# Causal masks of two attentions: 128 mask matmuls taken out, the mask moved to the scan and to GpSimd

## The chip, the cores and the metric

The kernel runs on one core of one Trainium2 chip. The metric is the device time of one execution in microseconds. The engines are named as in the profile: PE (TensorE, matmuls), PEld (its weight loads), DVE (VectorE), ACT (ScalarE), POOL (GpSimd) and SP (the queue that issues most DMAs).

## The reference

One decoder block on 1024 tokens of width 1024, in float32: eight heads of gated ("forgetting") attention and eight of stick-breaking attention side by side, attention to 256 memory tokens, and a convolutional gated FFN. Only the first part is touched:

```python
# gated heads, blocks of 128 queries
logits = q.k * scale + c[t] - c[s]          # c = cumsum(log f)
logits = where(s <= t, logits, -inf)
o = softmax(logits) @ v

# stick-breaking heads, strictly causal
z = q.k * scale
log_keep = where(s < t, log_sigmoid(-z), 0)
after = reverse_cumsum(log_keep) - log_keep  # over j > s
a = where(s < t, exp(log_sigmoid(z) + after), 0)   # sigmoid(z[t,s]) * prod_{s<j<t} (1 - sigmoid(z[t,j]))
o = a @ v
```

## The kernel before

Every float32 product is made of rounded parts: an operand is split into a high and a low part, ACT makes the high one and DVE the low one, and `mm3` (L201 to L203) adds three matmuls. The kernel has three stretches. From 0 to about 10 us it loads and normalises x. From there to about 612 us run the *planned steps*: both attentions, and between them, as background work for PE, the projections that make their queries, keys and values (`pq`, `pv`), those of the memory (`pk`, `pmv`) and half of the output projection (`pm`), which ends at about 640 us. Then come the rest of the output projection, the memory attention and the FFN.

The attention is cut into 32 groups: four pairs of heads (`pr`), for each first the gated kind ("f") and then the stick-breaking kind ("s"), two heads (`a`) and two halves of the queries (`g`). A group has four rows `i` of 128 queries; row `i` has 128 (i+1) keys, in chunks of at most 512. The steps of a row:

- `score` (L612, L613): two matmuls per chunk into a PSUM tile `st` (three of them). On the last chunk, which holds the diagonal block, a third matmul (L615) of a bfloat16 identity with a bfloat16 mask (0, or -1e30 above the diagonal) adds the mask to the last 128 columns.
- gated: `fox1` (L626) adds the gate row `negc` to the scores on DVE, writes them to SBUF as `p` and keeps the maximum in `fx`; L629 makes the negated maximum; `fox2` (L633) is the exponential on ACT with its sum; L588 the reciprocal on DVE; `fox3` (L636) the normalisation on POOL.
- stick-breaking: `sb1` (L644) and `sb2` (L647) are sigmoid(z) and sigmoid(-z) on ACT; `sb3` (L652) is a scan on DVE from the last column to the first, a running product that starts at 1; `sb4` (L658) multiplies sigmoid(z) by the scan shifted by one column, on POOL.

When its rows are done, a group turns them on PE (`turn`, L700), splits the result into high and low parts `pth` (L704) and `ptl` (L708), and multiplies by the values (`apply`, L716 and L717). Closing steps (L725 to L767) add the halves, split the result into `mh` and `ml` (which take tiles of `pth` and `ptl`) and store them.

The order of the work on each engine is written out by a planner: each step has an engine, a length, tiles that it takes and gives, and a due time `at`; a simulated run over these gives the order, and each engine then executes its own list, in that order, as the semaphores allow. One unit of due time is one group; `share` says how many us of background matmuls belong to each unit (about 8), `pace` deals them out, and R_STEP, T_OFF, T_LEN, W_LEAD and E_LEAD place the rows of a group, the turning, the loading of weights (`prep`: load L372, high L377, low L382) and the evacuations. The stretch ahead of the planned steps is ordered by a scheduler; there `get` (L189 to L195) loads and splits the first weights through three tiles `wraw`, and `norm_half` (L222 to L233) normalises two token tiles at a time and turns them on PE.

Of the kernel before, what the change touches and what calls it, by code (L numbers as in the profile page):

```python
# [133 lines left out]
def hybrid_block(ctx, tc, x, mem, w, wf, pcol, bfg, fing, out):  # L134
# [48 lines left out]
    def make_w(rp, wp):  # L183
        def get(i, eng=G):
            hi = wp.tile([P, 1024], F32R, tag="whi", name=f"whi{i}")
            lo = wp.tile([P, 1024], F32R, tag="wlo", name=f"wlo{i}")
            for c in (slice(0, 512), slice(512, 1024)):
                raw = rp.tile([P, 512], F32, tag="wraw", name=f"wraw{i}", bufs=3)
                in_turn("load", lambda: nc.sync.dma_start(raw, w[i, :, c]))  # L189
# [5 lines left out]
                in_turn("low", lambda: V.tensor_tensor(lo[:, c], raw, hi[:, c].bitcast(F32), op=ALU.subtract))  # L195
            return hi, lo
        return get
# [16 lines left out]
    def norm_half(src_tiles, gcol, hi, lo, pst, wk, n=4, tags=(("T", 2),), xtag="xn", eng=V):  # L214

        ss = small.tile([P, 4], F32, tag="ss", bufs=2, name="ss")
        rs = small.tile([P, 4], F32, tag="rs", bufs=2, name="rs")
        xn = []
        for j in range(n):
            xs = src_tiles[j]  # L220
            t = wk.tile([P, D], F32, tag=xtag, name="xn")
            A.activation(t, xs, AF.Square, accum_out=ss[:, j:j + 1])  # L222
            rsqrt_mean(rs[:, j:j + 1], ss[:, j:j + 1], 1, D)
            if eng is V:
                V.tensor_scalar(out=t, in0=xs, scalar1=rs[:, j:j + 1], scalar2=None, op0=ALU.mult)
# [52 lines left out]
    first_w = []  # L278
    hT = [half(0, 1, "h1_0"), half(2, 3, "h1_1")]
    with tc.tile_pool(name="nx", bufs=4, side="right", reuse_waits="tile") as nx:  # L280
        for th in range(2):
            xt = []
            for j in range(4):
                t = nx.tile([P, D], F32, tag="xin", name="xin")
                nc.sync.dma_start(t, x[(4 * th + j) * P:(4 * th + j + 1) * P, :])
                xt.append(t)
                if th == 0 and j % 2 == 1:
                    first_w.append(getw(ti))
# [4 lines left out]
            step = 2 if th else 2  # L293
            for j in range(0, 4, step):
                c = slice(j * P, (j + step) * P)
                norm_half(xt[j:j + step], C_ATTN, [t[:, c] for t in hT[th][0]], [t[:, c] for t in hT[th][1]],
                          ps, nx, n=step, tags=(("T", 2), ("S", 3)), eng=V if th == 0 else V)
# [11 lines left out]
        G.affine_select(out=mask_f, in_=zb, compare_op=ALU.is_ge, fill=NEG, base=0,  # L309
                        pattern=[[-1, P]], channel_multiplier=1)  # L310
        G.affine_select(out=mask_s, in_=zb, compare_op=ALU.is_ge, fill=NEG, base=-1,
                        pattern=[[-1, P]], channel_multiplier=1)
# [41 lines left out]
    def mm(n):  # L354
        return 30 * (n > 128) + n * 0.39 + 10
# [194 lines left out]
    negcs, kindend, before, stored, rms = {}, [], [None], {}, []  # L550

    class Group:
# [6 lines left out]
        def scores(self):  # L559
# [3 lines left out]
            for j in range(4):  # L563
# [7 lines left out]
                for n, (c0, w_) in enumerate(ch):  # L571
                    diag = c0 + w_ == n0
                    ms.append(plan.add(PE, 2 * mm(w_) + diag * mm(P), lambda i=i, c_=c_, n=n, c0=c0, w_=w_, diag=diag:
                                       self.score(i, c_, n, c0, w_, diag), need + ms,
# [4 lines left out]
                if kind == "f":  # L579
                    prev = [negcs[2 * pr + a]["in"]]  # L580
                    for n, (c0, w_) in enumerate(ch):
                        prev = [plan.add(DVE, 100 + dve(w_) + 130 * (n == len(ch) - 1),
                                         lambda i=i, c_=c_, n=n, c0=c0, w_=w_: self.fox1(i, c_, n, c0, w_),
                                         prev + [ms[n]], [],
                                         ["S"] + ["negc"] * (i == 7 and n == 1), at=at)]
                    e_ = plan.add(ACT, act(n0) + 95, lambda i=i, c_=c_, l=len(ch): self.fox2(i, c_, l), prev + kindend[-1:],
                                  at=at)
                    r_ = plan.add(DVE, 75, lambda c_=c_: V.reciprocal(c_["fx"][:, 3:4], c_["fx"][:, 3:4]), [e_], at=at)  # L588
                    o_ = plan.add(POOL, 100 + n0 * 1.05, lambda i=i, c_=c_: self.fox3(i, c_), [r_], [], ["fx"], at=at, lock=True)
                    last = e_  # L590
                else:
# [9 lines left out]
                    o_ = plan.add(POOL, 120 + n0 * 2.3, lambda i=i, c_=c_: self.sb4(i, c_), [s_] + pos, [], ["aw"], at=at,  # L601
# [6 lines left out]
        def score(self, i, c_, n, c0, w_, diag):  # L608
# [4 lines left out]
            T.matmul(st[:, :w_], lq, k2[:, c0:c0 + w_], start=False, stop=not diag)  # L613
            if diag:
                T.matmul(st[:, w_ - P:w_], identb, mask_f if self.kind == "f" else mask_s,  # L615
                         start=False, stop=True)
# [3 lines left out]

        def fox1(self, i, c_, n, c0, w_):
            if n == 0:
                self.row_tile(i, c_)
                c_["fx"] = small.tile([P, 4], F32, tag="fx", name="fx")
            mx, negc = c_["fx"][:, 0:2], negcs[2 * self.pr + self.a]["t"]
            V.tensor_tensor_reduce(out=c_["p"][:, c0:c0 + w_], in0=c_["st", n][:, :w_], in1=negc[:, c0:c0 + w_],  # L626
                                   scale=1.0, scalar=-3.0e38, op0=ALU.add, op1=ALU.max, accum_out=mx[:, n:n + 1])
            if c0 + w_ == P * (i + 1):
                V.tensor_scalar(out=c_["fx"][:, 2:3], in0=mx[:, 0:1], scalar1=mx[:, 1:2] if n else -3.0e38,  # L629
                                scalar2=-1.0, op0=ALU.max, op1=ALU.mult)  # L630

        def fox2(self, i, c_, l):
            A.activation(c_["p"], c_["p"], AF.Exp, bias=c_["fx"][:, 2:3], accum_out=c_["fx"][:, 3:4])  # L633

        def fox3(self, i, c_):
            G.tensor_scalar(out=c_["p"], in0=c_["p"], scalar1=c_["fx"][:, 3:4], scalar2=0.0,  # L636
# [12 lines left out]
        def sb3(self, i, c_, n, c0, w_):  # L649

            a, e = c_["a"], c0 + w_
            V.tensor_tensor_scan(out=a[:, c0:e][:, ::-1], data0=c_["st", n][:, :w_][:, ::-1],  # L652
                                 data1=ones.broadcast_to([P, w_]), initial=1.0 if e == P * (i + 1) else a[:, e:e + 1],
                                 op0=ALU.mult, op1=ALU.min)

        def sb4(self, i, c_):
            n0 = P * (i + 1)
            G.tensor_tensor(c_["p"][:, :n0 - 1], c_["p"][:, :n0 - 1], c_["a"][:, 1:], op=ALU.mult)  # L658

# [46 lines left out]
        def low(self, kb, n):  # L706
            t = self.sp["tl", kb] = sw.tile([P, 512], F32R, tag="ptl", name="ptl", bufs=NT)
# [30 lines left out]
        def end4(self):  # L738
            if len(self.hl) == 1:
                self.hl.append(sw.tile([P, 512], F32R, tag="ptl", name="ml", bufs=NT))  # L740
# [934 lines left out]
```

## Time and profile before

| | us |
|---|---|
| median of 3 runs | 1630.74 (1629.62 to 1633.43) |
| the profiled execution | 1631.46 |
| its span, first to last instruction | 1629.6 |
| PE busy in the span | 1547.3 (95%) |
| DVE busy | 1201.1 (74%) |
| ACT busy | 788.4 (48%) |
| POOL busy | 540.0 (33%) |

Busy time is the time in which an engine executes at least one instruction. Matmuls overlap in PE's pipeline, so the distance between the starts of two matmuls says more about what one costs than its recorded duration. Groups of instructions are shown with line, engine, operation, output and inputs, shape and count, then busy time, the mean of one in ns, and the idle time ahead of them with what ended it.

### The profile page before, as it was taken

What the parts mean: (1) busy time and instruction counts of PE and PEld (TensorE: products, weight loads), DVE (VectorE), ACT (ScalarE), POOL (GpSimd) and SP (SyncE); (2) the same over time, 40 slices, a digit from 0 to 9 for tenths busy, and PEclk for the clock granted to TensorE, in tenths of its full rate; (3) what the DMA queues carried; (4) which work ended last, traced back from release to release, by engine and by line L of the source; (5) the groups of instructions that cost most, each with busy time, mean ns of one, the idle gap of its engine ahead of it and who ended that gap; (6) DMA issues with size and microseconds to landing.
All of it is one profiled execution on the core that took longest, in us unless ns stands there. A gap on an engine that the chain in (4) does not pass through costs nothing. (4 is left out here: it accounts for less than half of the span.)

```text
span 1629.6 us, 22061 instructions
## 1 busy us (share of the span) xinstructions
PE 1547.3 (95%) x7812; PEld 1275.9 (78%) x7812; DVE 1201.1 (74%) x1952; ACT 788.4 (48%) x1546; POOL 540.0 (33%) x534
## 2 busy tenths in 40 slices
PE   7999999999999889999998987999999999999997
PEld 7678887887788767778886765877888888788886
DVE  7377777777867773365544979999999999786566
ACT  7368767767757660034334374333333333445444
POOL 2022313322321210123124439454554444133331
PEclk9999999999999999999999998999999999999999
DMA  5211021011113645512149731222222221998782
GB/s 178 104 53 66 27 65 65 27 53 65 40 53 130 233 142 188 174 45 73 52 139 209 134 119 52 94 87 80 89 78 83 86 91 65 323 296 204 150 189 104
DMA packets 76205, 183.53 MB, mean 113 GB/s; under 512 B 8376, under 2 KB 8504, under 8 KB 75840
## 3 DMA queue, kind: packets, MB, share of 16 engines
q1 hardware_dynamic: 61392, 151.58, 27.1%
q0 software_dynamic: 14400, 30.42, 10.3%
q8 instruction: 61, 1.00, 0.3%
q14 instruction: 48, 0.39, 0.1%
q10 hardware_dynamic: 304, 0.14, 0.0%
HBM read 129.64 MB, written 33.59 MB: 100 GB/s over the span
## 5 line engine op out<-in xcount | busy, mean ns | idle before, releaser
L658 POOL TENSOR_TENSOR p<-p,aw 128x383 f32<-128x383 f32 (+4 forms) x64 | 79.7, 1247 | 182.9 <-DVE aw L652 144.7
L708 DVE TENSOR_TENSOR ptl<-pt,pth 128x512 fp32r<-128x512 f32 x192 | 103.8, 549 | 36.4 <-ACT pth L704 35.0
L202 PE MATMUL dn<-opb,opa 128*128 128x512 f32 x308 | 120.5, 391 | 3.0 <-DVE opb L1133 3.0
L704 ACT ACTIVATE pth<-pt 128x512 fp32r<-128x512 f32 x192 | 92.5, 491 | 60.9 <-PE pt L700 56.9
L203 PE MATMUL dn<-opb,opa 128*128 128x512 f32 x308 | 120.3, 391 | 0.0
L636 POOL TENSOR_SCALAR p<-p,fx 128x128 f32<-128x128 f32 (+3 forms) x64 | 47.9, 753 | 212.1 <-DVE fx L588 166.3
L201 PE MATMUL dn<-opb,opa 128*128 128x512 f32 x308 | 117.9, 391 | 0.0
L700 PE MATMUL pt<-ident,p 128*128 128x128 f32 x576 | 96.6, 277 | 7.2 <-DVE ptl L708 7.1
L1284 POOL TENSOR_TENSOR tmp<-wv 128x512 f32<-128x512 f32 x21 | 43.1, 2050 | 162.6 <-DMA wv<-in_w_dram 153.1
L700 PEld LDWEIGHTS pt<-ident,p 128*128 128x128 f32 x576 | 70.4, 142 | 23.6 <-DVE ptl L708 12.0
L382 DVE TENSOR_TENSOR wlo<-wraw,whi 128x512 fp32r<-128x512 f32 x84 | 66.6, 825 | 24.8 <-ACT whi L377 23.4
L193 POOL TENSOR_SCALAR whi<-wraw 128x512 fp32r<-128x512 f32 x44 | 27.8, 645 | 154.2 <-PE pm L203 62.6
L1388 ACT ACTIVATE yv<-cv,pc 128x1024 f32<-128x1024 f32 x22 | 27.3, 1242 | 101.2 <-DVE cv L1420 93.1
L717 PE MATMUL po<-ptl,v 128*128 128x512 f32 x192 | 69.8, 364 | 5.1 <-DVE ptl L708 4.8
L377 ACT ACTIVATE whi<-wraw 128x512 fp32r<-128x512 f32 x84 | 49.7, 627 | 48.1 <-DMA wraw<-in_w_dram 22.7
L716 PE MATMUL po<-pth,v 128*128 128x512 f32 x192 | 71.1, 370 | 1.7 <-ACT k1f L465 1.5
L201 PE MATMUL up_p<-b,a 128*128 128x512 f32 x176 | 68.4, 392 | 4.1 <-DVE cg L1332 2.7
L202 PEld LDWEIGHTS dn<-opb,opa 128*128 128x128 f32 x308 | 58.2, 189 | 15.6 <-DVE opb L1133 3.5
L202 PE MATMUL up_p<-b,a 128*128 128x512 f32 x176 | 69.0, 392 | 0.0
L203 PE MATMUL up_p<-b,a 128*128 128x512 f32 x176 | 68.7, 391 | 0.0
L201 PEld LDWEIGHTS dn<-opb,opa 128*128 128x128 f32 x308 | 58.1, 189 | 12.1
L203 PEld LDWEIGHTS dn<-opb,opa 128*128 128x128 f32 x308 | 58.2, 189 | 12.0
(504 smaller groups left out, 5234.5 us busy)
## 6 DMA issues: line engine op xcount, KB each, us to landing
wraw<-in_w_dram SPq DMA_DIRECT2D x136, 256.0 KB, 3.0
a_d<-yv SPq DMA_DIRECT2D x22, 512.0 KB, 2.6
wv<-in_w_dram SPq DMA_DIRECT2D x21, 512.0 KB, 3.5
wg<-in_w_dram SPq DMA_DIRECT2D x20, 512.0 KB, 3.4
dn<-a_d POOLq DMA_DIRECT2D x32, 256.0 KB, 6.8
dn<-a_d SPq DMA_DIRECT2D x24, 256.0 KB, 9.8
dn<-in_w_dram SPq DMA_DIRECT2D x24, 256.0 KB, 8.6
xin<-in_x_dram SPq DMA_DIRECT2D x8, 512.0 KB, 5.2
```

Source lines behind the costliest of these rows:

```text
L201: T.matmul(o, lt[0], rt[0], start=start, stop=False)
L202: T.matmul(o, lt[0], rt[1], start=False, stop=False)
L203: T.matmul(o, lt[1], rt[0], start=False, stop=stop)
L377: A.activation(t["hi"][:, c], t["raw", n], AF.Copy)
L382: in_turn("low", lambda: V.tensor_tensor(t["lo"][:, c], t["raw", n], t["hi"][:, c].bitcast(F32), op=ALU.subtract))
L636: G.tensor_scalar(out=c_["p"], in0=c_["p"], scalar1=c_["fx"][:, 3:4], scalar2=0.0, op0=ALU.mult, op1=ALU.add)
L658: G.tensor_tensor(c_["p"][:, :n0 - 1], c_["p"][:, :n0 - 1], c_["a"][:, 1:], op=ALU.mult)
L700: T.transpose(pt[:, j * P:(j + 1) * P], self.rows[j]["p"][:, kb * P:(kb + 1) * P], ident)
L704: A.activation(t[:, 512 - n:], self.sp["pt", kb][:, 512 - n:], AF.Copy)
L708: V.tensor_tensor(t[:, 512 - n:], self.sp["pt", kb][:, 512 - n:], self.sp["th", kb][:, 512 - n:].bitcast(F32), op=ALU.subtract)
L716: T.matmul(self.po[:, c], lv, self.sp["th", kb][:, c], start=kb == 0, stop=False)
L717: T.matmul(self.po[:, c], lv, self.sp["tl", kb][:, c], start=False, stop=kb == 4 * self.g + 3)
```

## The change

The mask matmuls go. In the stick-breaking heads the scan starts from 0, and on the last chunk its second operand is a row of zeros and, in the last 128 columns, the identity (`zid`), with maximum in place of minimum: the running product is 0 down to the query's own column, is set to 1 there, and goes on from it. What stands above the diagonal is multiplied by 0, and the last column of `p`, which the shifted product doesn't reach, is cleared by a memset on POOL. In the gated heads POOL makes for each row a masked gate block `nm` (gate row plus mask, 128 x 128; two tiles) ahead of the scores, and `fox1` adds the plain gate row up to the diagonal block and `nm` on it, as two pieces where the chunk is wider than 128; the maximum becomes a reduction over one to three numbers.

The planner's figures change with it: R_STEP, T_LEN, W_LEAD, E_LEAD, the length of a 128-column matmul (120 ns instead of 60), the shares of the background; the low parts have three tiles instead of four. At the start the first weights' low parts are issued behind the first two normalised tiles, and two memsets of `k2f` go to POOL.

```diff
-    ident = const.tile([P, P], F32, name="ident")
+    zid = const.tile([P, 512], F32, name="zid")
+    ident = zid[:, 512 - P:]
     make_identity(nc, ident)
-    identb = const.tile([P, P], BF16, name="identb")
-    V.tensor_copy(identb, ident)
-    mask_f = const.tile([P, P], BF16, name="mask_f")
-    mask_s = const.tile([P, P], BF16, name="mask_s")
+    V.memset(zid[:, :512 - P], 0.0)
+    mask = const.tile([P, P], BF16, name="mask")
...
-                in_turn("low", lambda: V.tensor_tensor(lo[:, c], raw, hi[:, c].bitcast(F32), op=ALU.subtract))
+                def low(c=c, raw=raw):
+                    in_turn("low", lambda: V.tensor_tensor(lo[:, c], raw, hi[:, c].bitcast(F32), op=ALU.subtract))
+                if later is None:
+                    low()
+                else:
+                    later.append(low)
...
             xn.append(t)                       # norm_half, then=later for the first two token tiles
+        if then:
+            last_w["low"] = i_
+        for f in then:
+            f()
...
-    NT = 4
-    R_STEP, T_OFF, T_LEN, W_LEAD, E_LEAD = 0.28, 0.698, 0.655, 1.688, 0.101
-    plan = Plan({"P": 2, "S": 3, "T": 2, "O": 1, "th": NT, "tl": NT, "aw": 2, "ost": 2, "fx": 4, "raw": 3,
+    NT, NL = 4, 3
+    R_STEP, T_OFF, T_LEN, W_LEAD, E_LEAD = 0.296, 0.698, 0.645, 1.126, 0.136
+    plan = Plan({"P": 2, "S": 3, "T": 2, "O": 1, "th": NT, "tl": NL, "aw": 2, "ost": 2, "fx": 4, "raw": 3, "nm": 2,
...
     def mm(n):
-        return 30 * (n > 128) + n * 0.39 + 10
+        return max(120, 40 + n * 0.39)
...
                 if kind == "f":
-                    prev = [negcs[2 * pr + a]["in"]]
+                    prev = [plan.add(POOL, 250, lambda i=i, c_=c_: self.fox0(i, c_), [negcs[2 * pr + a]["in"]], ["nm"],
+                                     at=at - R_STEP, lock=True, behind=before[1])]
+                    before[1] = prev[0]
...
-        def score(self, i, c_, n, c0, w_, diag):
+        def score(self, i, c_, n, c0, w_):
             T.matmul(st[:, :w_], lq, k1[:, c0:c0 + w_], start=True, stop=False)
-            T.matmul(st[:, :w_], lq, k2[:, c0:c0 + w_], start=False, stop=not diag)
-            if diag:
-                T.matmul(st[:, w_ - P:w_], identb, mask_f if self.kind == "f" else mask_s,
-                         start=False, stop=True)
+            T.matmul(st[:, :w_], lq, k2[:, c0:c0 + w_], start=False, stop=True)
...
+        def fox0(self, i, c_):
+            c_["nm"] = sw.tile([P, P], F32, tag="nm", name="nm", bufs=2)
+            G.tensor_tensor(c_["nm"], negcs[2 * self.pr + self.a]["t"][:, i * P:(i + 1) * P], mask, op=ALU.add)
...
-            V.tensor_tensor_reduce(out=c_["p"][:, c0:c0 + w_], in0=c_["st", n][:, :w_], in1=negc[:, c0:c0 + w_],
-                                   scale=1.0, scalar=-3.0e38, op0=ALU.add, op1=ALU.max, accum_out=mx[:, n:n + 1])
-            if c0 + w_ == P * (i + 1):
-                V.tensor_scalar(out=c_["fx"][:, 2:3], in0=mx[:, 0:1], scalar1=mx[:, 1:2] if n else -3.0e38,
-                                scalar2=-1.0, op0=ALU.max, op1=ALU.mult)
+            def part(e0, e1, more):
+                V.tensor_tensor_reduce(out=c_["p"][:, e0:e1], in0=c_["st", n][:, e0 - c0:e1 - c0], in1=more,
+                                       scale=1.0, scalar=-3.0e38, op0=ALU.add, op1=ALU.max,
+                                       accum_out=c_["fx"][:, c_["parts"]:c_["parts"] + 1])
+                c_["parts"] += 1
+            d = i * P
+            if c0 < d:
+                part(c0, min(d, c0 + w_), negcs[2 * self.pr + self.a]["t"][:, c0:min(d, c0 + w_)])
+            if c0 + w_ == d + P:
+                part(d, d + P, c_["nm"])
+                V.tensor_reduce(out=c_["fx"][:, 3:4], in_=c_["fx"][:, :c_["parts"]], axis=AX.X, op=ALU.max,
+                                negate=True)
...
+            diag = e == P * (i + 1)
             V.tensor_tensor_scan(out=a[:, c0:e][:, ::-1], data0=c_["st", n][:, :w_][:, ::-1],
-                                 data1=ones.broadcast_to([P, w_]), initial=1.0 if e == P * (i + 1) else a[:, e:e + 1],
-                                 op0=ALU.mult, op1=ALU.min)
+                                 data1=zid[:, 512 - w_:][:, ::-1] if diag else zid[:, :1].broadcast_to([P, w_]),
+                                 initial=0.0 if diag else a[:, e:e + 1], op0=ALU.mult, op1=ALU.max)
...
             G.tensor_tensor(c_["p"][:, :n0 - 1], c_["p"][:, :n0 - 1], c_["a"][:, 1:], op=ALU.mult)
+            G.memset(c_["p"][:, n0 - 1:n0], 0.0)
...
-            V.memset(k2s[k][a][(1 - a) * HD:(2 - a) * HD, :].bitcast(F32), 0.0)
+            (G if k == "f" else V).memset(k2s[k][a][(1 - a) * HD:(2 - a) * HD, :].bitcast(F32), 0.0)
...
-    share = [QK + VAL]
-    for pr in range(3):
-        share += [FOX - (TAIL / 4 if pr == 0 else 0)] * 4 + [(QK * 2 + VAL - FOX * 4) / 4] * 4
-    share += [LAST[0]] * 4 + [LAST[1]] * 4
+    share = [QK + VAL] + [7.66, 7.66, 7.66, 7.66, 8.46, 8.46, 8.46, 8.46, 8.06, 8.06, 8.06, 8.06, 8.46, 8.46, 8.46, 8.46, 8.06, 8.06, 8.06, 8.06, 8.46, 8.46, 8.46, 8.46, 10.755, 10.755, 10.755, 10.755, 14.818, 14.818, 14.818, 14.818]
```

Before, QK, VAL, TAIL, FOX and LAST were 21.8, 22.5, 1.6, 8.044 and (11.147, 13.376).

More of the change, by code (lines that the diff above doesn't have):

```diff
@@ L183, in make_w, with get @@
     def make_w(rp, wp):
-        def get(i, eng=G):
+        def get(i, eng=G, later=None):
             hi = wp.tile([P, 1024], F32R, tag="whi", name=f"whi{i}")
@@ L212, in split, with norm_half @@
                                op0=ALU.mult, op1=ALU.subtract)
-    def norm_half(src_tiles, gcol, hi, lo, pst, wk, n=4, tags=(("T", 2),), xtag="xn", eng=V):
+    def norm_half(src_tiles, gcol, hi, lo, pst, wk, n=4, tags=(("T", 2),), xtag="xn", eng=V, then=()):
         ss = small.tile([P, 4], F32, tag="ss", bufs=2, name="ss")
@@ L224, in norm_half @@
             if eng is V:
-                V.tensor_scalar(out=t, in0=xs, scalar1=rs[:, j:j + 1], scalar2=None, op0=ALU.mult)
+                i_ = V.tensor_scalar(out=t, in0=xs, scalar1=rs[:, j:j + 1], scalar2=None, op0=ALU.mult).ins
             else:
@@ L277, in hybrid_block @@
     ps = att.enter_context(tc.tile_pool(name="ps", bufs=2, space=PSUM, reuse_waits="tile"))
-    first_w = []
+    first_w, later = [], []
     hT = [half(0, 1, "h1_0"), half(2, 3, "h1_1")]
@@ L287, in hybrid_block @@
                 if th == 0 and j % 2 == 1:
-                    first_w.append(getw(ti))
+                    first_w.append(getw(ti, later=later))
                     ti += 1
@@ L292, in hybrid_block @@
                 nc.scalar.dma_start(bf, bfg)
[L293 to L297, printed above, removed]
+            for j in (0, 2):
+                c = slice(j * P, (j + 2) * P)
+                norm_half(xt[j:j + 2], C_ATTN, [t[:, c] for t in hT[th][0]], [t[:, c] for t in hT[th][1]],
+                          ps, nx, n=2, tags=(("T", 2), ("S", 3)), then=later)
+                later = []
         xt = []
@@ L308, in hybrid_block @@
         V.memset(zb, 0.0)
-        G.affine_select(out=mask_f, in_=zb, compare_op=ALU.is_ge, fill=NEG, base=0,
-                        pattern=[[-1, P]], channel_multiplier=1)
-        G.affine_select(out=mask_s, in_=zb, compare_op=ALU.is_ge, fill=NEG, base=-1,
+        G.affine_select(out=mask, in_=zb, compare_op=ALU.is_ge, fill=NEG, base=0,
                         pattern=[[-1, P]], channel_multiplier=1)
@@ L548, in proj_mem @@
         return moved
-    negcs, kindend, before, stored, rms = {}, [], [None], {}, []
+    negcs, kindend, before, stored, rms = {}, [], [None, None], {}, []
     class Group:
@@ L571, in scores @@
                 for n, (c0, w_) in enumerate(ch):
[L572 to L574 removed]
+                    ms.append(plan.add(PE, 2 * mm(w_), lambda i=i, c_=c_, n=n, c0=c0, w_=w_:
+                                       self.score(i, c_, n, c0, w_), need + ms,
                                        ["S"] + [f"p{i}", "fx" if kind == "f" else "aw"] * (n == 0), at=at,
@@ L579, in scores @@
                 if kind == "f":
-                    prev = [negcs[2 * pr + a]["in"]]
+                    prev = [plan.add(POOL, 250, lambda i=i, c_=c_: self.fox0(i, c_), [negcs[2 * pr + a]["in"]], ["nm"],
+                                     at=at - R_STEP, lock=True, behind=before[1])]
+                    before[1] = prev[0]
                     for n, (c0, w_) in enumerate(ch):
-                        prev = [plan.add(DVE, 100 + dve(w_) + 130 * (n == len(ch) - 1),
+                        last = n == len(ch) - 1
+                        prev = [plan.add(DVE, 100 + dve(w_) + 130 * last + 175 * (last and w_ > P),
                                          lambda i=i, c_=c_, n=n, c0=c0, w_=w_: self.fox1(i, c_, n, c0, w_),
                                          prev + [ms[n]], [],
-                                         ["S"] + ["negc"] * (i == 7 and n == 1), at=at)]
+                                         ["S"] + ["nm"] * last + ["negc"] * (i == 7 and last), at=at)]
                     e_ = plan.add(ACT, act(n0) + 95, lambda i=i, c_=c_, l=len(ch): self.fox2(i, c_, l), prev + kindend[-1:],
                                   at=at)
-                    r_ = plan.add(DVE, 75, lambda c_=c_: V.reciprocal(c_["fx"][:, 3:4], c_["fx"][:, 3:4]), [e_], at=at)
+                    r_ = plan.add(DVE, 75, lambda c_=c_: V.reciprocal(c_["fx"][:, 4:5], c_["fx"][:, 4:5]), [e_], at=at)
                     o_ = plan.add(POOL, 100 + n0 * 1.05, lambda i=i, c_=c_: self.fox3(i, c_), [r_], [], ["fx"], at=at, lock=True)
@@ L600, in scores @@
                                       [ng[n]] + [s_] * (s_ is not None), [], ["S"], at=at)
-                    o_ = plan.add(POOL, 120 + n0 * 2.3, lambda i=i, c_=c_: self.sb4(i, c_), [s_] + pos, [], ["aw"], at=at,
+                    o_ = plan.add(POOL, 200 + n0 * 2.3, lambda i=i, c_=c_: self.sb4(i, c_), [s_] + pos, [], ["aw"], at=at,
                                   lock=True)
@@ L623, in fox1 @@
                 self.row_tile(i, c_)
-                c_["fx"] = small.tile([P, 4], F32, tag="fx", name="fx")
-            mx, negc = c_["fx"][:, 0:2], negcs[2 * self.pr + self.a]["t"]
-            V.tensor_tensor_reduce(out=c_["p"][:, c0:c0 + w_], in0=c_["st", n][:, :w_], in1=negc[:, c0:c0 + w_],
-                                   scale=1.0, scalar=-3.0e38, op0=ALU.add, op1=ALU.max, accum_out=mx[:, n:n + 1])
-            if c0 + w_ == P * (i + 1):
-                V.tensor_scalar(out=c_["fx"][:, 2:3], in0=mx[:, 0:1], scalar1=mx[:, 1:2] if n else -3.0e38,
-                                scalar2=-1.0, op0=ALU.max, op1=ALU.mult)
+                c_["fx"] = small.tile([P, 5], F32, tag="fx", name="fx")
+                c_["parts"] = 0
+            def part(e0, e1, more):
[10 more added lines that the diff above has]
+                                negate=True)
         def fox2(self, i, c_, l):
-            A.activation(c_["p"], c_["p"], AF.Exp, bias=c_["fx"][:, 2:3], accum_out=c_["fx"][:, 3:4])
+            A.activation(c_["p"], c_["p"], AF.Exp, bias=c_["fx"][:, 3:4], accum_out=c_["fx"][:, 4:5])
         def fox3(self, i, c_):
-            G.tensor_scalar(out=c_["p"], in0=c_["p"], scalar1=c_["fx"][:, 3:4], scalar2=0.0,
+            G.tensor_scalar(out=c_["p"], in0=c_["p"], scalar1=c_["fx"][:, 4:5], scalar2=0.0,
                             op0=ALU.mult, op1=ALU.add)
@@ L706, in low @@
         def low(self, kb, n):
-            t = self.sp["tl", kb] = sw.tile([P, 512], F32R, tag="ptl", name="ptl", bufs=NT)
+            t = self.sp["tl", kb] = sw.tile([P, 512], F32R, tag="ptl", name="ptl", bufs=NL)
             V.tensor_tensor(t[:, 512 - n:], self.sp["pt", kb][:, 512 - n:],
@@ L739, in end4 @@
             if len(self.hl) == 1:
-                self.hl.append(sw.tile([P, 512], F32R, tag="ptl", name="ml", bufs=NT))
+                self.hl.append(sw.tile([P, 512], F32R, tag="ptl", name="ml", bufs=NL))
             V.scalar_tensor_tensor(out=self.hl[1], in0=self.o, scalar=col(C_OUTG + self.kc),
```

## The prediction

> **What bounds the kernel now.** I read the page's head first, then the windows by stage, the waits of PE, and the matmuls in order of time around one mask. The windows give for each stretch the busy time of PE, of its weight loads (PEld), DVE, ACT and POOL, each with its count of instructions, then the granted clock.
>
> ```profile
> span 1629.6 us, 22061 instructions
> ...
> 10.00:612.00 602.00, 576.69 (x3453) 482.03 (x3454) 441.37 (x944) 409.57 (x896) 148.33 (x150) 0.99 0.24 83
> ...
> 190.00:255.00 65.00, 64.51 (x400) 54.89 (x399) 48.83 (x141) 45.28 (x99) 15.88 (x20) 1.00 0.17 58
> 255.00:314.00 59.00, 57.19 (x334) 46.59 (x332) 45.50 (x72) 46.91 (x101) 18.13 (x14) 1.00 0.14 46
> ...
> 612.00:640.00 28.00, 24.49 (x102) 19.32 (x101) 10.13 (x15) 3.05 (x5) 0.00 (x0) 0.96 0.52 170
> ```
>
> The change lies in the stretch from 10 to 612 us, where the planned steps run; 612 to 640 is the end of the planned projections. In the 602 us PE is busy 576.69, DVE 441.37 (73%), ACT 409.57 (68%), POOL 148.33 (25%), at a clock of 0.99. 190 to 255 is a gated ("f") stage, 255 to 314 a stick-breaking ("s") one; both have PE at 97% or more, DVE at 75 to 77%.
>
> ```profile
> PE pt L700 <- DVE ptl L708: 7.1, 8, 2.0
> PE po L717 <- DVE ptl L708: 4.8, 10, 2.0
> PE pk L201 <- DVE mk L528: 3.1, 1, 3.1
> PE pm L201 <- ACT whi L377: 2.9, 1, 2.9
> ```
>
> These are PE's four longest waits from 10 to 640 us (total, times, longest). PE waits for little, and mostly for the low parts that DVE makes (L708). A busy share may flatter PE, since matmuls overlap; so I look at the distance between starts.
>
> ```profile
> 255.12 0.39 PE L612 MATMUL st<-k1s,qs 128*128 128x512 f32 x1
> 255.35 0.40 PE L613 MATMUL st<-k2s,qs 128*128 128x512 f32 x1
> 255.58 0.23 PE L615 MATMUL st<-mask_s,identb 128*128 128x128 bf16 x1
> 255.62 0.47 PE L201 MATMUL pq<-h_0h,whi 128*128 128x512 f32 x1
> 255.94 0.39 PE L202 MATMUL pq<-h_0l,whi 128*128 128x512 f32 x1
> ...
> 256.86 0.39 PE L201 MATMUL pq<-h_0h,whi 128*128 128x512 f32 x1
> 257.09 0.40 PE L202 MATMUL pq<-h_0l,whi 128*128 128x512 f32 x1
> ```
>
> Without a mask a 512-column matmul starts 0.23 us after the one before (257.09 - 256.86). So this is a queue with work in it: PE sets the pace here.
>
> **The masks that go.** With the mask, L202 starts 255.94 - 255.35 = 0.59 us after the second score product; two plain steps would be 0.46. One mask costs 0.13 us: 0.04 of its own and 0.09 because the next weights come later.
>
> ```profile
> L615 PE MATMUL st<-mask_s,identb 128*128 128x128 bf16 x64 | 14.8, 231 | 0.0
> L615 PE MATMUL st<-mask_f,identb 128*128 128x128 bf16 x64 | 14.7, 230 | 0.0
> L615 PEld LDWEIGHTS <-identb 128*128 128x128 bf16 x128 | 12.3, 96 | 15.2 <-issue 13.8
> ```
>
> There are 64 + 64 of them. Worked out in this way from the starts around each of the 128, the median is 0.126 us: 128 x 0.126 = 16.1 us of PE. The bounds are 12.3 us (their weight loads alone) and 29.5 us (14.8 + 14.7, their whole recorded durations). I take 16.1, which is measured between starts.
>
> **The gated rows on DVE.** Rows of L626 by width, the read of its accumulator, and the step that made the negated maximum:
>
> ```profile
> L626 DVE CUSTOM_DVE_ANT_0 p<-st,negc 128x512 f32<-128x512 f32 x48 | 32.9, 685 | 7.3 <-PE st L613 4.8 <-PE st L615 1.7 <-PE po L716 0.6
> L626 DVE CUSTOM_DVE_ANT_0 p<-st,negc 128x384 f32<-128x384 f32 x16 | 8.8, 550 | 1.6 <-PE st L615 0.9 <-PE po L716 0.6
> L626 DVE DVE_READ_ACCUMULATOR2_ANT fx<- 128x1 f32 x96 | 7.9, 83 | 0.1
> L629 DVE TENSOR_SCALAR fx<-fx 128x1 f32<-128x1 f32 x64 | 11.8, 184 | 2.2
> L626 DVE CUSTOM_DVE_ANT_0 p<-st,negc 128x256 f32<-128x256 f32 x16 | 6.7, 416 | 0.9 <-PE st L615 0.6 <-POOL p L636 0.3
> L626 DVE CUSTOM_DVE_ANT_0 p<-st,negc 128x128 f32<-128x128 f32 x16 | 4.6, 290 | 3.4 <-PE st L615 3.1
> ```
>
> The last chunk of a row is split into the columns before the diagonal block and the block itself. Of 64 rows, 16 end in a 128-wide chunk and stay one piece; 48 become two. A 512 chunk was 685 ns; 384 and 128 are 550 + 290, and one more accumulator read is 83: +238 ns; the other widths give +239 and +247. That is 48 x 0.24 = 11.6 us more DVE. The maximum is now a reduction over one to three numbers in place of L629's 184 ns; the trace has none so small. Its bounds are the 83 ns and the 290 ns here, 64 x (-0.10 to +0.11) = -6.5 to +6.8 us; as nearest to L629 I take 184 again, 0. So DVE goes from 441.4 to 453 us, in a stage of about 590: 77%. Between none (it fits DVE's idle time) and all 11.6 on the path, I take 4 us: the rows above have PE seldom behind DVE, but in a gated stage DVE rises from 75% to about 81%, and then its low parts are late more often.
>
> [...]
>
> **What GpSimd gets.**
>
> ```profile
> 0.24 0.10 POOL L1664 MEMSET const-float32-0.0<- 128x1 f32 x1 [0.24 <-issue]
> ...
> L658 POOL TENSOR_TENSOR p<-p,aw 128x127 f32<-128x127 f32 x8 | 3.3, 412 | 17.6 <-DVE aw L652 17.6
> ...
> POOL p L636 <- DVE fx L588: 166.3, 38, 52.7
> POOL p L658 <- DVE aw L652: 144.7, 52, 9.2
> ...
> L382 DVE TENSOR_TENSOR wlo<-wraw,whi 128x512 fp32r<-128x512 f32 x84 | 66.6, 825 | 24.8 <-ACT whi L377 23.4
> ...
> L382 DVE TENSOR_TENSOR wlo<-wraw,whi x84: 656/685/2485, 41.3 to 636.9; 128x512 fp32r<-128x512 f32 x84
> ```
>
> A masked gate block is a 128x128 sum: 64 x 0.41 = 26.4 us. A cleared last column is a 128x1 memset: 64 x 0.10 = 6.4 us. POOL goes from 148 to 181 us, 31% of the stage, and what it waits for is DVE, for 311 us here. The gate block has a new wait, for its tile (two of them), which DVE frees; behind it in POOL's queue stand the products L658 and the normalisations L636, which PE's transposes wait for. But DVE is to free that tile before it makes the reciprocal for which L636 waits. The memset stands after L658 and makes that row's transposes 0.1 us later, under background matmuls. POOL also meets DVE: a low part of a weight (L382) has taken 656 to 2485 ns, so it can be held up for a whole POOL instruction. POOL is busy 33/148 = 22% more of the time; if the excess of L382's group (84 times its mean of 825 ns less its least of 656: 14 us) grows in step, that is +3 us of DVE. Bounds for all of POOL's part: 0 and 33 us; nearest are the long waits, in which it hides. I take 0.5 us.
>
> ```profile
> L652 DVE TENSOR_TENSOR_SCAN aw<-st,aw,ones 128x512 f32<-128x512 f32 x32 | 40.8, 1274 | 0.3
> L652 DVE TENSOR_TENSOR_SCAN aw<-st,ones 128x512 f32<-128x512 f32 x16 | 19.5, 1216 | 2.2 <-ACT st L647 1.8 <-issue 0.3
> ```
>
> The scan keeps its count and widths. Its second operand becomes a real row in 64 of 96. It takes 1216/512 = 2.4 ns a column, while L626 above reads such a second stream at 685/512 = 1.3 ns; so I take 0, with bounds of -1 and +3 us (64 x 50 ns, about the difference of these two rows, whose sources differ).
>
> **Pace, buffers, start.** The shares rise by 4 x (10.755 + 14.818 - 11.147 - 13.376) = 4.2 us of projection work, which moves from 612-640 into the last s stage. PE's work stays the same; where it fills one of PE's gaps it gains up to 4.2 us, else 0. I take 0. Weights are fetched 1.126 steps of some 8 us (the shares) ahead instead of 1.688, 9 us instead of 13.5. The other leads move score rows by 0.13 us each (0.016 steps) and evacuations by 0.3 us (0.035 steps) in the order: 0, with PE's waits above as what they could lengthen.
>
> ```profile
> wraw<-in_w_dram SPq DMA_DIRECT2D x136, 256.0 KB, 3.0
> ...
> mix_d<-ml SPq DMA_DIRECT2D x2, 256.0 KB, 4.4
> ```
>
> A weight half lands in 3.0 us. Its load goes out later on SP, where the same loads and stores as before stand behind it, and ACT's and DVE's conversions move with it; cost 0, hidden by the rest of the 9 us, and if the cover goes, PE waits as at L377 above, 2.9 us at a time. Low-part tiles go from four to three, the price of the gate blocks' room; 14 times a closing part `ml` holds one until its store lands, 4.4 us. Bounds 0 and 14 x 2.0 us (the longest wait on L708); I take 0, since two tiles serve one written and one read.
>
> ```profile
> 7.68 0.75 DVE L225 TENSOR_SCALAR xn<-xin,rs 128x1024 f32<-128x1024 f32 x1
> 8.36 0.68 DVE L195 TENSOR_TENSOR wlo<-wraw,whi 128x512 fp32r<-128x512 f32 x1
> 8.95 1.10 DVE L225 TENSOR_SCALAR xn<-xin,rs 128x1024 f32<-128x1024 f32 x1
> 9.06 0.33 SPq L189 DMA_DIRECT2D wraw<-in_w_dram  x1
> ```
>
> At the start four low parts go behind the second normalised tile, which so starts at most 0.6 us sooner (8.95 - 8.36). The fourth weight half has the first one's tile: its load, now at 9.06, goes out after the deferred low part, 1.7 us later, with the loads of x queued behind it on SP. Two memsets move from DVE to POOL, idle then. Between -0.6 and +1.7 us I take 0.
>
> **Sum**, against the profiled execution's own 1631.46 us (0.72 over the median of 1630.74): 1631.46 - 16.1 + 4 + 0.5 = 1619.9, so 1620 us.
>
> **Rivals.**
> 1. More: all of DVE's part is hidden and the 4.2 us fill gaps (612 to 640 has PE idle for 3.5): 1631.5 - 16.1 - 4.2 = 1611. For it: DVE is idle for 160 us of the stage. Against: PE's waits are on DVE already.
> 2. DVE takes it back: 11.6 + 3 of DVE, all on the path: 1631.5 - 16.1 + 14.6 = 1630. It needs DVE to be the last to end nearly everywhere; PE's waits above speak against it.
> 3. PE is not the bound: its weight loads fill 482.03 of 602 us, 80%; then a matmul less leaves a gap and the time stays at 1631. Start distances of 0.23 us speak against it. [...]
> 4. Slower: the third low-part tile. If each of the 14 closings leaves PE without a tile for 2.0 us, 28 us come and 16.1 go: 1631.5 - 16.1 + 4 + 28 = 1647; it decides from (16.1 - 4) / 14 = 0.9 us a closing on. For it: L717 and L700 wait for `ptl` now, with four. Against: those waits are 12 us in all.
>
> **How the numbers follow.** My forecast has 0.60 (its own range 1613 to 1627), rival 1 0.13, rival 2 0.08, rival 3 0.06, rival 4 0.13. About 0.2% (3.3 us) is what a measurement of this kernel can tell. Faster: 0.60 + 0.13 = 0.73; same: 0.08 + 0.06 = 0.14; slower: 0.13. The range takes in rivals 1 to 3 and leaves out the slower one and some beyond 1606: 1606 to 1633.
>
> **What would show it.** No L615; PE's count down by 128, its stretch up to the last `po` shorter by 10 to 14 us, and after it nothing changed. 48 more L626 pieces, DVE's busy time in the stage about 12 us up. 64 POOL sums near 0.41 us. PE's waits on `ptl` up by some 4 us; if they rise by 15, rival 2 or 4 holds: 4 where they lie behind `ml`. If PE's gaps widen by what the masks took, rival 3.

## The result and the profile after

The changed kernel took 1623.05 us (median of 4 runs, 1618.8 to 1623.69) against 1630.48 before: ratio 0.9946, interval 0.9929 to 0.9962. A second set (experiment 4) gave 0.9929 (0.9909 to 0.9949). So it is some 7 to 12 us faster, as forecast; but three terms of the sum had the wrong size, and that their errors cancelled is luck.

The windows of the changed kernel: us, then busy time and count of PE, PEld, DVE, ACT and POOL, the granted clock, and DMA. By the first scores of each stage, the gated stage runs here from 188.4 to 246.8 us and the stick-breaking one from 246.8 to 308.3; before they ran from 189.5 to 248.6 and 248.6 to 310.9. So the prediction's windows, 190 to 255 and 255 to 314, are some 4 to 6 us off the stages; the busy shares of PE and DVE that it reads there move by a point at most when the windows are set right.

```profile
span 1617.0 us, 22066 instructions
...
10.00:612.00 602.00, 573.05 (x3374) 488.51 (x3374) 449.28 (x1046) 409.50 (x896) 178.47 (x278) 0.99 0.25 86
...
188.00:247.00 59.00, 58.13 (x356) 50.35 (x355) 45.96 (x156) 39.76 (x90) 20.90 (x35) 1.00 0.18 59
247.00:308.00 61.00, 57.93 (x325) 48.13 (x325) 49.37 (x72) 48.66 (x107) 20.01 (x31) 1.00 0.14 48
```

The last product with the values (`po`) starts at 599.4 us, before at 609.2; the span is 12.6 us shorter, and 9.8 us of it are gone by then. PE looks as busy as before, POOL has 30 us more. The new instructions, from the groups by shape:

```profile
L631 POOL TENSOR_TENSOR nm<-negc,mask 128x128 f32<-128x128 f32 x64 | 28.1, 443 | 109.8 <-DVE fx L640 66.4 <-DMA negc<-negc_d 43.3
...
L640 DVE CUSTOM_DVE_ANT_0 p<-st,nm 128x128 f32<-128x128 f32 x64 | 18.2, 285 | 0.8 <-PE st L623 0.6 <-PE pt L723 0.2
...
L681 POOL MEMSET p<- 128x1 f32 x64 | 6.3, 98 | 0.0
L650 DVE TENSOR_REDUCE fx<-fx 128x1 f32<-128x2 f32 x32 | 5.0, 155 | 1.1
L674 DVE TENSOR_TENSOR_SCAN aw<-st,zid 128x512 f32<-128x512 f32 x16 | 19.5, 1218 | 4.4 <-ACT st L668 4.3
```

Prices are near the forecast: 443 ns for a gate block (412 assumed), 98 for a memset (100), 285 for a piece (290), 155 for the small maximum (184), and the scan is unchanged at 1218 (1216). PE's waits, 10 to 640 us:

```profile
PE po L740 <- DVE ptl L731: 10.5, 9, 4.1
PE pt L723 <- DVE ptl L731: 7.3, 7, 4.1
PE pm L207 <- ACT whi L385: 2.7, 1, 2.7
```

The waits on `ptl` went from 11.9 to 17.8 us. And a score without its mask, in order of time:

```profile
254.49 0.39 PE L623 MATMUL st<-k2s,qs 128*128 128x512 f32 x1
254.71 0.39 PE L207 MATMUL pq<-h_0h,whi 128*128 128x512 f32 x1
254.94 0.39 PE L208 MATMUL pq<-h_0l,whi 128*128 128x512 f32 x1
```

From L623 to L208 it is 0.45 us, where it was 0.59: at this place the matmul and the late weights behind it are gone (the load of L208's weights starts 0.01 us after L207, at 254.72; before, that of L202's 0.09 us after L201, at 255.71).

### The profile page after: what moved, and what is told of

It reads as the page before. It is cut to its first block, busy times and chain, and to the rows that moved or that the text cites. A ratio compares the mean times of both kernels' runs of the same rounds, so it can differ in the third digit from the quotient of the medians.

```text
span 1617.0 us, 22066 instructions
## 1 busy us (share of the span) xinstructions
PE 1532.5 (95%) x7684; PEld 1273.8 (79%) x7684; DVE 1203.7 (74%) x2046; ACT 788.1 (49%) x1546; POOL 570.5 (35%) x663
## 3 DMA queue, kind: packets, MB, share of 16 engines
q1 hardware_dynamic: 61392, 151.58, 27.1%
## 5 line engine op out<-in xcount | busy, mean ns | idle before, releaser
L208 PE MATMUL dn<-opb,opa 128*128 128x512 f32 x308 | 120.4, 391 | 2.0 <-DVE opb L1153 2.0
L207 PE MATMUL dn<-opb,opa 128*128 128x512 f32 x308 | 118.1, 391 | 0.0
L723 PE MATMUL pt<-zid,p 128*128 128x128 f32 x576 | 96.2, 276 | 7.8 <-DVE ptl L731 7.3
L723 PEld LDWEIGHTS pt<-zid,p 128*128 128x128 f32 x576 | 72.7, 142 | 27.0 <-DVE ptl L731 9.3
L390 DVE TENSOR_TENSOR wlo<-wraw,whi 128x512 fp32r<-128x512 f32 x84 | 67.8, 834 | 21.9 <-ACT whi L385 21.3
L740 PE MATMUL po<-ptl,v 128*128 128x512 f32 x192 | 69.5, 362 | 10.9 <-DVE ptl L731 10.5
L1408 ACT ACTIVATE yv<-cv,pc 128x1024 f32<-128x1024 f32 x22 | 27.3, 1242 | 100.0 <-DVE cv L1440 92.8
L207 PE MATMUL up_p<-b,a 128*128 128x512 f32 x176 | 68.4, 392 | 4.1 <-DVE cg L1352 2.8
L208 PEld LDWEIGHTS dn<-opb,opa 128*128 128x128 f32 x308 | 58.3, 189 | 14.3 <-DVE opb L1153 2.4
L208 PE MATMUL up_p<-b,a 128*128 128x512 f32 x176 | 69.0, 392 | 0.0
L207 PEld LDWEIGHTS dn<-opb,opa 128*128 128x128 f32 x308 | 58.2, 189 | 12.2
```

Of the source, the lines that this page charges most:

```text
L207: T.matmul(o, lt[0], rt[0], start=start, stop=False)
L208: T.matmul(o, lt[0], rt[1], start=False, stop=False)
L390: in_turn("low", lambda: V.tensor_tensor(t["lo"][:, c], t["raw", n], t["hi"][:, c].bitcast(F32), op=ALU.subtract))
L723: T.transpose(pt[:, j * P:(j + 1) * P], self.rows[j]["p"][:, kb * P:(kb + 1) * P], ident)
L740: T.matmul(self.po[:, c], lv, self.sp["tl", kb][:, c], start=False, stop=kb == 4 * self.g + 3)
```

## The experiments

All ratios are to the kernel before on the same chip, with their 95% interval behind them. Every run but 1, 8 and 10 keeps both causal masks.

**1. The masks gone, nothing in their place.** On the kernel before:

```diff
-            T.matmul(st[:, :w_], lq, k2[:, c0:c0 + w_], start=False, stop=not diag)
-            if diag:
-                T.matmul(st[:, w_ - P:w_], identb, mask_f if self.kind == "f" else mask_s, start=False, stop=True)
+            T.matmul(st[:, :w_], lq, k2[:, c0:c0 + w_], start=False, stop=True)
```

> The kernel before without its 128 mask matmuls (L615) and with nothing in their place, so the causal mask is left out in both attentions; planner and orders of all engines as before. Theory (PE sets the pace): the whole 16.1 us go, 1613 to 1617 us against 1630.5 before; PE's idle time between 10 and 612 us stays near its 25 us. Rival (PE is not the bound): 1628 to 1631 us, and PE's waits grow by 12 us or more.

Measured: 0.9971 (0.9957 to 0.9984), 4.7 us; neither theory. Two thirds of the 16.1 us don't come out. PE's waits in this kernel:

```profile
PE pt L697 <- DVE ptl L705: 7.8, 9, 2.0
PE po L714 <- DVE ptl L705: 7.0, 13, 2.8
```

14.8 us against 11.9: that explains 3 us. The rest is in gaps which the list of waits does not count. Two rows of the kernel before show why:

```profile
132.76 0.22 PE L716 MATMUL po<-pth,v 128*128 128x128 f32 x1
133.17 0.33 PE L717 MATMUL po<-ptl,v 128*128 128x128 f32 x1 [0.18 <-DVE ptl L708]
```

The first has 128 columns, and the median step between this pair is 0.06 us; here it is 0.41. The list counts 0.18 of these 0.35 us, as the first one's recorded 0.22 reach over the rest. So I took all starts of matmuls from 20 us to the last `po`. From each step (the distance between two starts) I took what the shortest tenth of the steps between the same two kinds and widths needs, and called the rest *late* (masks_gone_free is this kernel, change_again experiment 4, change_masks_back 9, pace_alone 2):

| us | matmul steps | late by under 0.15 | by 0.15 to 0.5 | by more | sum |
|---|---|---|---|---|---|
| before | 507.8 | 44.4 | 10.9 | 26.2 | 589 |
| masks_gone_free | 500.5 | 40.7 | 13.9 | 29.7 | 585 |
| change (first profile) | 502.4 | 38.5 | 9.2 | 29.3 | 579 |
| change_again | 502.8 | 39.0 | 12.4 | 27.3 | 581 |
| change_masks_back | 510.7 | 42.9 | 6.4 | 27.1 | 587 |
| pace_alone | 510.3 | 45.9 | 13.4 | 35.8 | 605 |

How the shortest tenth is taken moves 2 to 4 us between the first two columns; the sums stay. PE was late by 81 us in the 589, not by the 25 that the waits add up to. But the 81 are not all waits for others. Of the 44 us that are late by under 0.15, some 29 lie in steps right behind a 128-column matmul, 9 behind masks and 17 to 19 behind transpositions: there the next weights come later, as behind the mask in the prediction. In the trace of before, where a 512-column matmul follows a mask (53 places) or a transposition of 128 columns (137), the next load starts 0.083 us after that matmul and the step takes 0.31 to 0.32 us; where it follows another 512-column matmul (1038), 0.003 and 0.23 (medians). What could hide a mask is the 37 us of the next two columns.

In masks_gone_free 7.3 + 3.7 = 11 us of the first two columns go, and 3.0 + 3.5 us of longer waits come. As both kernels have the same matmuls in the same order but for the masks, each step can also be set against its own twin. At the 128 places of the masks the two steps concerned are 11.9 us shorter in all: 0.12 us at the median, but 0.07 at the 40 places where transpositions or the products `po` follow. Everywhere else the steps are 6.8 us longer in sum, 3.6 of them where PE waits for `ptl`; the rest is spread over many places. Net 5.1 us, beside the 4.7 measured. Two profiles of one and the same kernel (the change, here and in experiment 4) differ by 2.1 us in this way, so the 6.8 is good to about 2.

**2. The pace alone.** The kernel before with the new R_STEP, T_LEN, W_LEAD, E_LEAD, `mm` and `share`.

> The kernel before with its masks, but with the new planner figures (R_STEP, T_LEN, W_LEAD, E_LEAD, mm and the shares). Theory (the gain is the masks'): 1628 to 1635 us. Rival (the pace gives the gain): 1622 to 1626 us.

1.0063 (1.0047 to 1.0078): 10 us *slower*, outside both. With the masks in, the new figures make PE late by 95 us in the profiled execution. That one is the longest of the six (1647.51 us; the median is 1643.43), and some 5 of its 14 us of added lateness are clock (an estimate, half of the difference between two times): in its planned steps the clock stands at half for 23.9 us, before for 13.7. Single waits of 5 and 6 us stand out:

```profile
PE pt L700 <- DVE ptl L708: 10.7, 9, 5.0
PE po L716 <- ACT pth L704: 6.5, 2, 6.0
```

**3. The change at the old pace**, the same figures put back in the changed kernel.

> The changed kernel with the planner figures of before (R_STEP, T_LEN, W_LEAD, E_LEAD, mm and the shares). Theory (the gain is the masks', less some 4 to 8 us that DVE takes back): 1620 to 1627 us. Rival (the pace gives the gain): 1629 to 1633 us.

0.9976 (0.9964 to 0.9988), 4 us. Applied to the 1630.5 us of before this is 1626.6, at the upper end of the first range; the 1629.79 us measured stand beside 1634.47 for the kernel before on this chip. Without any replacement, experiment 1 gave 0.9971 and experiment 8 gives 0.9962. So what the change adds on DVE and POOL costs 1 to 2 us at this pace, less than the intervals can tell from nothing, and the new pace is worth some 5 to 8 us more, though only with the masks gone.

**4. The change once more.**

> The changed kernel once more, to narrow its interval. All theories: 1619 to 1624 us. If the granted clock explains the 5 us between its own runs (1618.8 to 1623.7), the slower executions show a lower clock, some 0.003 for 5 us.

0.9929, with the median at 1620.84 (six runs, 1619.31 to 1629.27). On the clock, see the last section.

**5 to 7. Parts of the pace.** In the changed kernel one part each goes back to its old value: `share`; `W_LEAD` (1.688); R_STEP, T_LEN, E_LEAD and `mm`.

> The changed kernel with the shares of background work of before (and the new leads and matmul length). The pace as a whole is worth some 8 us of the change (ratio 0.9929 with it, 0.9976 without). Theory A (the shares are what counts: they say how much background stands between two groups): ratio 0.997 to 0.998, as with the whole old pace. Theory B (the shorter lead of the weights is what counts): 0.993, as with the new pace.

> The changed kernel with the weights' lead of before (1.688 instead of 1.126 steps). Theory A (shares): ratio 0.992 to 0.994. Theory B (weights' lead: early conversions on ACT and DVE stand ahead of low parts that PE waits for): 0.996 to 0.998.

> The changed kernel with R_STEP, T_LEN, E_LEAD and the matmul length of before. Theories A and B: ratio 0.992 to 0.994. Theory C (the rows' spacing and the turning's length count: they set when a row's DVE steps stand against the low parts): 0.996 to 0.998.

0.9962 (0.9950 to 0.9974), 0.9973 (0.9962 to 0.9985) and 0.9940 (0.9925 to 0.9955). Theories A and B each hold for their own part, A a little less than it forecast, and fail for the other's: going back on either loses over half of what the new pace gave. The lead's loss is the less certain one, as its twelve runs had a mean clock of 0.9828 beside 0.9842 for the kernel before. With the spans of all runs brought to one clock, at 1.2 us for a thousandth (last section), the change (experiment 4) is 11.5 us ahead of before, 4.0 with the whole old pace, 6.5 with the old shares, 7.3 with the old lead and 9.3 with the old small figures, each to about 1.5 us. The small figures (C) are worth at most some 2 us, which can't be told from nothing.

**8. The masks gone, and the planner told** (`2 * mm(w_) + diag * mm(P)` becomes `2 * mm(w_)` as well).

> The kernel before without mask matmuls and with nothing in their place (the causal mask is left out), as in masks_gone_free, but the planner's score steps are shortened too, so the orders are made anew for the shorter scores; the pace is the old one. Theory D (the old order was made for a PE with masks, and the freed 16 us turn into waits only because of it): ratio 0.991 to 0.994. Theory A, B or C (the figures of the pace hold it back): 0.996 to 0.998, as without it.

0.9962 (0.9947 to 0.9976), against 0.9971 untold: the intervals overlap, so D isn't shown; a new simulated order alone doesn't bring the 16 us.

**9. Mask matmuls put back into the change**, as products of zeros:

```diff
-            T.matmul(st[:, :w_], lq, k2[:, c0:c0 + w_], start=False, stop=True)
+            diag = c0 + w_ == P * (i + 1)
+            T.matmul(st[:, :w_], lq, k2[:, c0:c0 + w_], start=False, stop=not diag)
+            if diag:
+                T.matmul(st[:, w_ - P:w_], zid[:, :64].bitcast(BF16), zid[:, 64:128].bitcast(BF16), start=False, stop=True)
```

> The changed kernel with 128 matmuls of 128 bfloat16 columns put back where the masks were (zeros times zeros, so they add nothing); the planner is not told, so every engine's order is that of the change. Theory S (PE has waits of its own between matmuls, some 75 us in the planned steps, and part of the masks fits into them): 5 to 9 us over the change, ratio 0.996 to 0.999. Theory P of the prediction (PE sets the pace): 16 us over it, ratio 1.002 to 1.004.

0.9987 (0.9973 to 1.0001) against 0.9946 and 0.9929 without: 7 to 9 us, theory S; the interval leaves out theory P. Its matmuls in order of time:

```profile
257.63 0.40 PE L624 MATMUL st<-k2s,qs 128*128 128x512 f32 x1
257.87 0.23 PE L626 MATMUL st<-zid 128*128 128x128 bf16 x1
257.91 0.47 PE L207 MATMUL pq<-h_0h,whi 128*128 128x512 f32 x1
258.22 0.39 PE L208 MATMUL pq<-h_0l,whi 128*128 128x512 f32 x1
```

Here it costs its 0.13 us again (258.22 - 257.63 = 0.59). But in the table the waits of 0.15 to 0.5 us fall from 12.4 to 6.4: about 12 us of matmul time come (7.9 + 3.9), and half of it lies where PE stood anyway. Twin by twin, as in experiment 1, the steps at the 128 places are 11.4 us longer than in the change's repeat and 12.5 longer than in its first profile, and all other steps together 5.7 and 5.2 us shorter.

**10. The gated heads' block for free**: `fox0` issues nothing, `fox1` is not split.

> The changed kernel without POOL's masked gate blocks and without the split of the last chunk, so the gated heads have no causal mask; the planner still counts both, so the orders stay. It takes 48 pieces (11.6 us) from DVE and 64 sums (28 us) from POOL. Prediction (4 of the 11.6 us lie on the path, 0.5 us for POOL): ratio 0.990 to 0.9915 (the change: 0.993). Rival (all of DVE's 11.6 us on the path): 0.986. Rival (all hidden): 0.993.

0.9936 (0.9917 to 0.9955), as the change itself: all hidden, as far as can be told (beside the 0.9929 of experiment 4, a gain of over some 3.4 us is ruled out). DVE's busy time on the page says why. First the change (the run of experiment 4), then this one:

```profile
PE 1535.1 (95%) x7684; PEld 1275.1 (79%) x7684; DVE 1203.8 (74%) x2046; ACT 788.4 (49%) x1546; POOL 566.4 (35%) x663
```

```profile
PE 1536.6 (95%) x7684; PEld 1274.9 (79%) x7684; DVE 1200.3 (74%) x1950; ACT 787.4 (48%) x1546; POOL 541.3 (33%) x599
```

48 pieces and their 48 reads of the accumulator are worth 3.5 us of DVE, not 11.6: the recorded durations overlap. Row by row, one 256-wide end of a row before and after:

```profile
93.29 0.42 DVE L626 CUSTOM_DVE_ANT_0 p<-st,negc 128x256 f32<-128x256 f32 x1
93.64 0.08 DVE L626 DVE_READ_ACCUMULATOR2_ANT fx<- 128x1 f32 x1
93.75 0.21 DVE L629 TENSOR_SCALAR fx<-fx 128x1 f32<-128x1 f32 x1
```

```profile
93.16 0.29 DVE L640 CUSTOM_DVE_ANT_0 p<-st,negc 128x128 f32<-128x128 f32 x1
93.38 0.08 DVE L640 DVE_READ_ACCUMULATOR2_ANT fx<- 128x1 f32 x1
93.38 0.28 DVE L640 CUSTOM_DVE_ANT_0 p<-st,nm 128x128 f32<-128x128 f32 x1
93.59 0.08 DVE L640 DVE_READ_ACCUMULATOR2_ANT fx<- 128x1 f32 x1
93.70 0.16 DVE L650 TENSOR_REDUCE fx<-fx 128x1 f32<-128x3 f32 x1
```

0.67 us then (93.29 to 93.96), 0.70 now (93.16 to 93.86). The second piece starts together with the read, 0.07 us ahead of the first one's recorded end. Over all rows the median from the first piece's start to the maximum's end is 957 ns for 384 + 128 and 876 for the unsplit 512 of this experiment, 691 and 613 for 128 + 128 and 256: 0.08 us a split. Against the kernel before it is less still, as the new maximum is shorter: 957 beside 910 for the 512-wide end, 691 beside 643, and 484 beside 538 where nothing is split.

**11. Three tiles for the low parts, in the kernel before.**

> The kernel before with three tiles for the low parts (ptl, ml) instead of four. Prediction (two tiles serve): ratio 0.999 to 1.001. Rival 4 (a closing leaves PE without a tile, 2.0 us each): up to 1.017; from 0.9 us a closing on, 1.008.

0.9999 (0.9981 to 1.0016), and the waits on `ptl` are as before. Rival 4 has no price.

```profile
PE pt L700 <- DVE ptl L708: 7.1, 8, 2.0
PE po L717 <- DVE ptl L708: 4.7, 11, 1.4
```

**12. A still shorter lead of the weights**, 0.9 steps.

> The changed kernel with the weights' lead shortened further, from 1.126 to 0.9 steps (1.688 gave 0.9973, 1.126 gave 0.993). Theory B (the earlier the conversions, the more they stand ahead of low parts that PE waits for): ratio 0.990 to 0.993, a version that beats both. Rival (there is a best lead, and below it PE waits for the weights): 0.995 to 1.000, with more waits of PE on whi and wlo than the 5 us of the change.

0.9968 (0.9955 to 0.9981): no gain over 1.126, and PE doesn't wait longer for the weights either. Both accounts fail:

```profile
PE po L740 <- DVE ptl L731: 7.8, 11, 2.6
PE pt L723 <- DVE ptl L731: 7.5, 7, 4.1
PE pv L207 <- DVE k2f L482: 4.2, 2, 3.6
PE pm L207 <- ACT whi L385: 2.8, 1, 2.8
PE pq L207 <- ACT whi L385: 2.2, 1, 2.2
```

That 0.9 is the worse lead isn't shown. The profiled execution is level with that of experiment 4 through all the planned steps (the last `po` starts at 601.7 and 601.5 us, the FFN's first `up_p` at 940.9 and 941.0), and its 3.2 us more come in the FFN, where the two kernels are alike; besides, its ten runs had a mean clock of 0.9823, the kernel before 0.9843 beside them, and brought to one clock their spans are 7.9 us ahead of before. Why 1.126 is better than 1.688 stays open. What is shown is that the old shares cost some 5 us and the old lead some 4, in these two cases by no single wait that explains it. No version that was run beats the change.

## Why the prediction was right, point by point

- **"PE sets the pace here."** Half right, and the step that failed. It rested on a list of waits of 25 us in 602 and on start distances in one busy place. By the starts of all matmuls PE was late by 81 of 589 us, 37 of them in steps late by 0.15 us or more. PE is 96% busy (576.69 of 602 us) and 14% late in the same trace. Rival 3, at 0.06, held for half to two thirds of the masks' time.
- **The masks, -16.1 us.** Two errors. The term took the median, 0.126 us, for all 128; set against their twins they are worth 11.9 us, as a third of them cost 0.07 (experiment 1). And not all of that shows in the time: 4.7 us measured at the old orders (1), 7 to 9 at the new ones (9). The shortened queue waits longer elsewhere, in experiment 1 for over half of it where it needs low parts. The term was mis-sized by about a factor of two to three.
- **DVE's pieces, 11.6 us of work and +4 on the path.** 3.5 us of work, and nothing on the path that can be told (10); up to the last `po` DVE is busy for 443.54 us, before for 440.30. The forecast added recorded durations that overlap; from the first piece's start to the maximum's end it is 48 x 0.08 = 3.8 us. The small maximum takes 155 ns (184 taken).
- **POOL, +0.5 us.** 28.1 + 6.3 = 34.4 us of work (32.8 forecast). The new wait for the gate block's tile is there, 66.4 us, and harmless: experiment 10 takes 28 us from POOL without effect. POOL does hold up the weights' low parts on DVE (L382, now L390): before, the 61 that overlap no POOL instruction took at most 694 ns, the 23 that do 1194 at the mean and 2485 at most; now 52 took at most 694 and 32 took 1078 at the mean. But the +3 us that was feared for DVE doesn't show: the group goes from 66.6 us to 67.8.
- **Pace, 0.** The largest miss after the masks: some 5 to 8 us of the gain (3), from shares and weights' lead (5, 6). I read these figures as moves of equal work; they set the orders in which the engines meet, and have opposite signs with and without the masks (2).
- **Low-part tiles, scan: 0**, as forecast (11, and 1218 against 1216 ns). The 4.4 us for a store of `ml` were those of the last two; over all 14 the median is 2.0.
- **Start, 0.** The fourth weight half's load goes out at 10.38 us instead of 9.06, the first projection starts at 10.90 instead of 11.25, and the first score at 77.3 instead of 76.8: nothing is left of it.
- **The sum, 1620 us**, stands beside 1618.8 (profiled run) and 1623.05, because -16.1 + 4.5 came out near -4 - 6: too much for the masks and for what replaces them, nothing for the pace. The right total is luck. Of the signs named ahead, the stretch up to the last `po` is 9.8 us shorter (10 to 14 named), but 2.8 us more are gone behind it, where nothing was to change, and DVE's 12 us are 3.

## What to carry to other kernels

Here a PE that was 96% busy was late for 81 of 589 us, some 29 of them right behind 128-column matmuls. Before costing removed matmuls at their full step, sum the steps between starts against the shortest ones of the same shapes: the list of waits had 25 of the 81 us, as a wait can lie under the recorded length of the matmul before (0.18 of 0.35 us counted in the pair of experiment 1). Add up the cost of all the places (11.9 us), not the median times their number (16.1). Where a trial kernel keeps the order, set its steps against their twins. Price a split instruction from start to end of the sequence (0.08 us here), not by adding recorded durations (0.24). Where the order of the work is planned by hand, removing work and moving the plan are one change: here each alone gave -5 and +10 us, and both together -7 to -12.

## What the runs showed of the hardware

A good part of the scatter between runs of one kernel goes with the granted TensorE clock. The changed kernel's four runs had spans of 1617.0, 1621.0, 1621.9 and 1621.5 us at mean clocks of 0.986, 0.984, 0.983 and 0.983. In the 81 runs of the kernel before that stand beside the experiments the mean span was 1632.4 us at 0.983 (19 runs), 1631.1 at 0.984 (22), 1630.3 at 0.985 (23) and 1626.7 at 0.987 (5). From 0.983 to 0.987 that is 5.7 us, 1.4 us for a thousandth of the clock; a line through all 81 runs, chip by chip, gives 1.2. A thousandth of 1630 us is 1.6 us, so by this slope some three quarters of the clock that was lost was time lost. In the traces it is lost in whole pieces: in the planned steps of the kernel before the clock stands at half for 3.4 us from 81.2, for 3.4 from 545.4 and for 6.8 from 600.0, in the changed kernel's first profile for 3.4 from 536.3 and for 6.8 from 587.5, and at full between. From 10 to 620 us of the kernel before, the step between two 512-column matmuls is 0.43 us at the median in these pieces (11 steps) and 0.23 outside them (1074). At an equal 0.985 the change's repeat had a span of 1618.8 us against 1630.3, so differences of 3 us between single runs should be read only beside their clocks. The spans and clocks of the two profiled executions, before first:

```profile
core 0: 1629.6 us, clock 0.985
```

```profile
core 0: 1617.0 us, clock 0.986
```
